# A macaron decoder trunk on one core: attention as a pipeline of score groups, with half of the last conv group's taps queued on VectorE behind the last window block's scaling

## Chip, core and metric

One core of a Trainium2 chip runs the whole program. The metric is the device time of one execution in microseconds. The profile's engines are PE (TensorE matmuls), PEld (TensorE weight loads), DVE (VectorE), ACT (ScalarE), POOL (GpSimd) and SP (the queue that issues most DMAs).

## What is computed

Two layers (L = 2) over a sequence of 512 tokens with 1024 channels. Each layer is a half-step feed-forward block, a mixer, and another half-step feed-forward block, each behind an RMS norm. Only the mixer is touched here:

```python
p = rms_norm(h) @ w_in                       # columns: conv (2 x 384), q (6 heads), k, v (2 heads), q_mem (4 heads)
u, gate = split(conv columns)
y_conv = silu(layer_norm(causal_depthwise_conv31(u * sigmoid(gate)) + b))
q, k = rope(rms_norm(q)), rope(rms_norm(k))
y_swa = softmax([q k^T / 8 + band mask, sink])[:-1] @ v     # sliding window of 128, in blocks of 128 queries
y_mem = softmax(rms_norm(q_mem) mk^T / 8) @ mv              # 256 memory tokens, mk and mv once per layer
h = h + concat(y_conv, y_swa, y_mem) @ w_out
```

## The kernel before

All data are float32. Large products are done as three fp32r products of a high and a low part (`mm3`, L172 to L174): the operand's high part is a copy by ScalarE (L141), its low part a subtraction by VectorE (L142). Small products (scores, probabilities by values, transposes) are plain fp32; a plain fp32 product appears on TensorE as two instructions, a transpose as one.

A tile framework records the operations of the source and orders them per engine by a timeline of its own; every engine then works through its own queue strictly in that order. `with queued():` and `tc.issue_after(x)` bind an instruction to stand behind `x` on its engine's queue; `tail[0]` holds the last TensorE instruction that such a binding refers to.

The mixer of a layer runs these steps (`ORDER`, L45), written in this order: `c0 c1 q v c2 r0 r1 w0 w1 w2 r2 w3 r3 t0 t1 t2 s`.

- `c` (`conv_in`, L631): for one of three groups of 128 conv channels, two projections of 24 matmuls of 512 columns (value half and gate half), then on VectorE the scaling by the RMS factor `R` and the gating into `ypad` (L646 to L649).
- `q` and `v` (`queries`, `values`): four tiles of 128 tokens each. For q, k and the memory queries a chain follows: ScalarE squares, VectorE sum of squares (L526), L527, GpSimd's power (L189), VectorE's scaling per head (L531), then transposes on TensorE (L555) and a copy by ScalarE (L557).
- `w` (`window`, L721) and `r` (`recall`, L740), one call for each block of 128 queries: a pair of heads at a time, scores (L728 and L745), the row minimum on VectorE (L731 with the mask added, L746 without), exponential with a sum of the row on ScalarE (L697), transposes of the probabilities (L702), a copy (L704), the product with the values (L707). At the end of a block the division by the sum (L713), transposes (L716) and the split into `y` (L141, L142). The keys of the two heads lie in one zero-padded tile (`kz`, `mz`), so that a score product has all 128 rows as contraction and 512 columns.
- `t` (`taps`, L752): for each group one tensor_scalar (L753) and 30 scalar_tensor_tensor operations of 128x512 (L756) on VectorE. The scheduler puts these between the other operations of VectorE.
- `s` (`swish`, L760): sum of the three groups on GpSimd (L762, L763), mean on TensorE (L765), its subtraction (L768), squares, their column sums on TensorE (L197), the power on GpSimd, its spreading over the tokens (L210), then scaling, Silu and split into `y[0]` to `y[2]`.

The output projection comes behind: eight blocks `d` of 15 matmuls that take the attention parts `y[3]` to `y[7]`, in eight PSUM banks, then eight blocks of 9 matmuls that take the conv parts, L794, and the next norm's operand. `whi` and `wlo` have four buffers each.

Of the kernel before, what the change touches and what calls it, by code (L numbers as in the profile page):

```python
# [18 lines left out]
P = 128  # L19
D = 1024  # L20
S = 512
# [22 lines left out]
MAGIC = 12582912.0  # L44
ORDER = "c0 c1 q v c2 r0 r1 w0 w1 w2 r2 w3 r3 t0 t1 t2 s"  # L45

# [13 lines left out]
def trunk(ctx: ExitStack, tc: tile.TileContext, xT, memT, pos, w1a, w3a, w2a, w1b, w3b, w2b,  # L60
# [15 lines left out]
    def queued():  # L76

        return tc.issue_after(tail[0].ins)
# [100 lines left out]
    def blk(k, n=P):  # L179
        return slice(k * n, (k + 1) * n)  # L180
# [89 lines left out]
    class Seven:  # L270
# [37 lines left out]
        def rest(self):  # L308
# [9 lines left out]
            self.cut(4, f)  # L318

    def gated():  # L320

        p = (gp.tile([P, 2, S], F32R, tag="ghi", name="ghi"), gp.tile([P, 2, S], F32R, tag="glo", name="glo"))
        return [at(p, ALL, i, ALL) for i in range(2)]
# [187 lines left out]

    mz = res.tile([P, 2, 2, MEM], F32, name="mz")
    for i in range(2):
        G.memset(mz[blk(1 - i, HD), :, i, :], 0.0)
    mvn = res.tile([P, 2, 256], F32, name="mvn")
    rmem = const.tile([P, 2], F32, name="rmem")
# [43 lines left out]
    def memory(l):  # L560
# [20 lines left out]
        for t in range(2):  # L581
            A.activation(mvn[:, t, :], pp[t][:, 256:512], AF.Copy, scale=rmem[:, t : t + 1])
# [5 lines left out]
            pt = to_columns(None, q, 2, "mm")  # L588
            for i in range(2):
                e = blk(i, HD)  # L590
                A.activation(mz[e, :, i, blk(t)], pt[e], AF.Copy, scale=-(HD**-0.5))

# [6 lines left out]
    def mixer(l, x, st, last):  # L599
# [6 lines left out]
        qT = here[:, 0:1536].rearrange("p (c s) -> p c s", c=CC)  # L606
        kz = here[:, 1536:2560].rearrange("p (i s) -> p i s", i=2)
        vn = here[:, 2560:3072].rearrange("p (t e) -> p t e", t=NT)
        qmT = there[:, 0:1024].rearrange("p (i s) -> p i s", i=2)
        cv = there[:, 1024:2560].rearrange("p (c s) -> p c s", c=CC)  # L610
        for i in range(2):
            G.memset(kz[blk(1 - i, HD), i, :], 0.0)
        scratch = [wst.tile([P, UNIT], F32, tag="aux", name=f"aux{i}", bufs=3) for i in range(3)]
# [11 lines left out]

        y = [z for _ in range(KD // 2) for z in gated()]


        R, rc = None, const.tile([P, NT], F32, tag="rc", name="rc")

        def conv_in(c):  # L631
            nonlocal R
            pp = []
            for i in range(2):
                with queued() if 2 * c + i < 3 else nullcontext():
                    ps = mm()
                    project(ps, weights(wconv[l, c, i], 1024, V), x)
                    pp.append(ps)
                if c == 0:
                    with queued():  # L640
                        if i == 0:
                            V.tensor_copy(rc, rms_cols(st, D))
                        else:
                            R = kept(spread(rc), "R")
            u, s = ypad[:, c, PAD:], ring("cv")
            V.tensor_tensor(out=u, in0=pp[0], in1=R, op=ALU.mult)  # L646
            V.tensor_tensor(out=s, in0=pp[1], in1=R, op=ALU.mult)
            A.activation(s, s, AF.Sigmoid)
            V.tensor_tensor(out=u, in0=u, in1=s, op=ALU.mult)  # L649


        def queries():
            ww = [weights(wqk[l, i], 1024, G) for i in range(4)]
            for t in range(NT):
# [18 lines left out]
                pt = to_columns(qT[:, :, blk(t)], q, 4)  # L673
                for i in range(2):
                    e = blk(i, HD)
                    A.activation(kz[e, i, blk(t)], pt[e, CC, :], AF.Copy, scale=-(HD**-0.5))


        def values():
            ww = [weights(wvm[l, i], 768, V) for i in range(4)]  # L680
            for t in range(NT):
                ps = mm()
                for k in range(KD):
                    mm3(ps[:, 0:CCH], at(x, ALL, k, blk(t)), at(ww[k // 2], ALL, blk(k % 2, CCH)), k == 0, k == KD - 1)
                A.activation(vn[:, t, :], ps[:, 256:CCH], AF.Copy, scale=rc[:, t : t + 1])
# [6 lines left out]
        def weighted(c, nk, scores, nm, den, values, po):  # L692

            pr = ring("pr").rearrange("p (i k) -> p i k", i=2)
            for i in range(2):
                n = 2 * c + i
                A.activation(pr[:, i, 0 : nk * P], scores[:, i, 0 : nk * P], AF.Exp, bias=nm[:, n : n + 1], scale=-1.0,  # L697
                             accum_out=den[:, n : n + 1])
            pt = bank([P, 2, 2, P], "pt")
            for i in range(2):  # L700
                for j in range(nk):
                    T.transpose(pt[:, i, j, :], pr[:, i, blk(j)], ident)  # L702
            ptb = ring("ptb").rearrange("p (i j q) -> p i j q", i=2, j=2)
            A.activation(ptb[:, :, 0:nk, :], pt[:, :, 0:nk, :], AF.Copy)  # L704
            for i in range(2):
                for j in range(nk):
                    T.matmul(po[:, 2 * c + i, :], ptb[:, i, j, :], values(j, i), start=(j == 0), stop=(j == nk - 1))  # L707

        def attended(b, c0, c1, po, rd):

            n = 2 * (c1 - c0)
            z = ring("yn")[:, 0 : (c1 - c0) * P]
            V.tensor_tensor(out=heads(z), in0=po, in1=rd.unsqueeze(2).to_broadcast([P, n, HD]), op=ALU.mult)  # L713
            pt = bank([P, c1 - c0, P], "cf")
            for c in range(c1 - c0):
                T.transpose(pt[:, c, :], z[:, blk(c)], ident)  # L716
            for c in range(c1 - c0):
                hi, lo = at(y[CC + c0 + c], ALL, blk(b))
                split(hi, lo, pt[:, c, :], V)

        def window(b):  # L721
            nk = 2 if b else 1
            b0, W = b - nk + 1, nk * P
            nm, es, den, rd = (sm(NH, f"a{n}", "a", 12) for n in range(4))
            po = bank([P, NH, HD], "po")
            for c in range(CC):
                ps = bank([P, 2, 256], "mm")
                T.matmul(ps[:, :, 0:W], qT[:, c, blk(b)], kz[:, :, b0 * P : b0 * P + W], start=True, stop=True)  # L728
                for i in range(2):
                    n = 2 * c + i  # L730
                    V.tensor_tensor_reduce(out=ps[:, i, 0:W], in0=ps[:, i, 0:W], in1=mask[:, 256 - W : 256], scale=1.0,  # L731
                                           scalar=nsink[:, l, n : n + 1], op0=ALU.add, op1=ALU.min, accum_out=nm[:, n : n + 1])
                weighted(c, nk, ps, nm, den, lambda j, i: vn[:, b0 + j, blk(i, HD)], po)
            V.tensor_tensor(out=es, in0=sink, in1=nm, op=ALU.add)
            A.activation(es, es, AF.Exp)
            V.tensor_tensor(out=den, in0=den, in1=es, op=ALU.add)
            V.reciprocal(rd, den)
            attended(b, 0, CC, po, rd)

        def recall(b):  # L740
            nm, den, rd = (sm(NM, f"m{n}", "a", 12) for n in range(3))
            po = bank([P, NM, HD], "po")
            for c in range(2):
                ps = bank([P, 2, 256], "mm")
                T.matmul(ps, qmT[:, c, blk(b)], mz[:, c], start=True, stop=True)  # L745
                V.tensor_reduce(out=nm[:, 2 * c : 2 * c + 2], in_=ps, axis=AX.X, op=ALU.min)  # L746
                weighted(c, 2, ps, nm, den, lambda j, i: mvn[:, j, blk(2 * c + i, HD)], po)
            V.reciprocal(rd, den)
            attended(b, CC, CC + 2, po, rd)


        def taps(c):  # L752
            V.tensor_scalar(out=cv[:, c, :], in0=ypad[:, c, 0:S], scalar1=conv_w[:, c, 0:1], scalar2=conv_b[:, c : c + 1],  # L753
                            op0=ALU.mult, op1=ALU.add)
            for j in range(1, TAPS):
                V.scalar_tensor_tensor(out=cv[:, c, :], in0=ypad[:, c, j : j + S], scalar=conv_w[:, c, j : j + 1],  # L756
                                       in1=cv[:, c, :], op0=ALU.mult, op1=ALU.add)

# [19 lines left out]
        for step in ORDER.split():  # L778
            f = {"c": conv_in, "q": queries, "v": values, "w": window, "r": recall, "t": taps, "s": swish}[step[0]]
            f(*map(int, step[1:]))  # L780
# [141 lines left out]
```

## Time and profile before

| quantity | value |
|---|---|
| median of 3 runs | 1829.91 us (1829.8 to 1833.07) |
| profiled execution | 1829.19 us |
| its span | 1827.4 us, mean granted TensorE clock 0.993 |
| busy: PE, PEld, DVE, ACT, POOL | 97%, 86%, 72%, 49%, 10% of the span |
| mixer of the first layer, values to the end of attention | 442.9 to 516.4 us |
| mixer of the second layer, the same | 1344.4 to 1415.3 us |

The profiled execution is 1.8 us longer than its span (work around the span) and 0.7 us under the median. Rows of the timeline read: start, duration, engine, source line, operation, output <- inputs, shape, count; in brackets the idle time of the engine ahead of the row and what ended it. Rows overlap, since an instruction starts before the one ahead of it has left the pipeline; what an instruction costs its engine is therefore the distance from start to start.

### The profile page before, as it was taken

What the parts mean: (1) busy time and instruction counts of PE and PEld (TensorE: products, weight loads), DVE (VectorE), ACT (ScalarE), POOL (GpSimd) and SP (SyncE); (2) the same over time, 40 slices, a digit from 0 to 9 for tenths busy, and PEclk for the clock granted to TensorE, in tenths of its full rate; (3) what the DMA queues carried; (4) which work ended last, traced back from release to release, by engine and by line L of the source; (5) the groups of instructions that cost most, each with busy time, mean ns of one, the idle gap of its engine ahead of it and who ended that gap; (6) DMA issues with size and microseconds to landing.
All of it is one profiled execution on the core that took longest, in us unless ns stands there. A gap on an engine that the chain in (4) does not pass through costs nothing.

```text
span 1827.4 us, 28061 instructions
## 1 busy us (share of the span) xinstructions
PE 1773.5 (97%) x10892; PEld 1579.3 (86%) x10892; DVE 1306.6 (72%) x1990; ACT 887.8 (49%) x1453; POOL 177.8 (10%) x182
## 2 busy tenths in 40 slices
PE   8999999999899999999999999999988999999997
PEld 6889999878577989898888898988776889898986
DVE  8967666579957867576678685666799477675755
ACT  4546444354646535353555463535356455353532
POOL 3001000014101000000010010000240010000000
PEclk9999999999999999999999999999999999999998
DMA  7356655162038456565565475643420576474622
GB/s 244 105 171 171 166 138 151 53 170 76 8 91 204 103 152 160 142 169 142 147 141 153 147 177 138 168 119 102 109 83 13 135 161 162 133 180 122 172 76 81
DMA packets 91285, 243.63 MB, mean 133 GB/s; under 512 B 9360, under 2 KB 11664, under 8 KB 91152
## 3 DMA queue, kind: packets, MB, share of 16 engines
q1 hardware_dynamic: 77040, 190.45, 34.0%
q0 software_dynamic: 14112, 51.39, 15.9%
q8 instruction: 86, 1.41, 0.3%
q14 instruction: 47, 0.39, 0.1%
HBM read 239.70 MB, written 2.10 MB: 132 GB/s over the span
## 4 chain that ended last, share of the span: by engine, by line
PE 77%; DVE 11%; issue 7%; DMA 2%; ACT 2%; POOL 0%; SPq 0%; DVEq 0%; POOLq 0%; ACTq 0%
PE mm L172 11%; PE mm L173 11%; PE mm L174 11%; PE po L172 8%; PE po L173 8%; PE po L174 8%; PE pt L173 5%; PE pt L172 5%; PE pt L174 5%; DVE there L756 4%; DVE wlo L142 1%; DMA wsum<-in_w3b 1%; DVE mm L731 1%; DVE xlo L152 1%; PE cf L172 1%
## 5 line engine op out<-in xcount | busy, mean ns | idle before, releaser
L141 ACT ACTIVATE whi<-raw 128x1024 fp32r<-128x1024 f32 (+4 forms) x384 | 353.1, 924 | 514.1 <-PE mm L173 248.1
L142 DVE TENSOR_TENSOR wlo<-raw,whi 128x1024 fp32r<-128x1024 f32 (+4 forms) x384 | 404.6, 1056 | 128.0 <-ACT whi L141 127.0
L173 PE MATMUL mm<-glo,whi 128*128 128x512 f32 x752 | 294.1, 391 | 0.0
L174 PE MATMUL mm<-ghi,wlo 128*128 128x512 f32 x752 | 293.4, 390 | 0.0
L172 PE MATMUL mm<-ghi,whi 128*128 128x512 f32 x752 | 289.8, 392 | 0.8 <-ACT ghi L141 0.8
L174 PE MATMUL po<-mh,wlo 128*128 128x256 f32 x864 | 244.6, 283 | 1.3 <-DVE wlo L142 1.3
L172 PE MATMUL pt<-xhi,whi 128*128 128x256 f32 x864 | 243.3, 283 | 2.7 <-ACT xhi L141 2.0
L172 PE MATMUL po<-mh,whi 128*128 128x256 f32 x864 | 244.8, 283 | 0.8 <-ACT part L377 0.8
L173 PE MATMUL pt<-xlo,whi 128*128 128x256 f32 x864 | 243.7, 283 | 1.5 <-DVE xlo L142 1.5
L173 PE MATMUL po<-ml,whi 128*128 128x256 f32 x864 | 244.6, 283 | 0.0
L174 PE MATMUL pt<-xhi,wlo 128*128 128x256 f32 x864 | 243.7, 283 | 0.0
L455 DVE SCALAR_TENSOR_TENSOR h<-mm,h 128x512 f32<-128x512 f32 x128 | 87.8, 688 | 139.1 <-PE mm L174 139.0
L172 PEld LDWEIGHTS pt<-xhi,whi 128*128 128x128 f32 x864 | 165.1, 192 | 4.2 <-ACT xhi L141 2.4
L172 PEld LDWEIGHTS mm<-ghi,whi 128*128 128x128 f32 x752 | 141.6, 189 | 30.6 <-ACT ghi L141 1.3
L173 PEld LDWEIGHTS pt<-xlo,whi 128*128 128x128 f32 x864 | 165.7, 192 | 2.5 <-DVE xlo L142 1.7
L172 PEld LDWEIGHTS po<-mh,whi 128*128 128x128 f32 x864 | 165.8, 192 | 1.8 <-ACT part L377 1.2
L174 PEld LDWEIGHTS po<-mh,wlo 128*128 128x128 f32 x864 | 165.8, 192 | 1.6 <-DVE wlo L142 1.6
L174 PEld LDWEIGHTS mm<-ghi,wlo 128*128 128x128 f32 x752 | 141.6, 188 | 29.4
L173 PEld LDWEIGHTS po<-ml,whi 128*128 128x128 f32 x864 | 165.8, 192 | 0.6
L173 PEld LDWEIGHTS mm<-glo,whi 128*128 128x128 f32 x752 | 141.7, 188 | 28.3 <-DVE glo L142 0.4
L174 PEld LDWEIGHTS pt<-xhi,wlo 128*128 128x128 f32 x864 | 165.5, 192 | 0.0
L756 DVE SCALAR_TENSOR_TENSOR there<-ypad,par,there 128x512 f32<-128x512 f32 x180 | 134.1, 761 | 0.7
(271 smaller groups left out, 3256.4 us busy)
## 6 DMA issues: line engine op xcount, KB each, us to landing
raw<-in_w2a SPq DMA_DIRECT2D x48, 384.0 KB, 3.5
raw<-in_w2b SPq DMA_DIRECT2D x48, 384.0 KB, 3.8
raw<-in_w1b SPq DMA_DIRECT2D x26, 512.0 KB, 3.7
raw<-in_w3b SPq DMA_DIRECT2D x26, 512.0 KB, 3.7
raw<-in_w1a SPq DMA_DIRECT2D x25, 512.0 KB, 3.7
raw<-in_w3a SPq DMA_DIRECT2D x25, 512.0 KB, 4.1
wsum<-in_w1a SPq DMA_DIRECT2D x18, 512.0 KB, 4.5
wsum<-in_w3a SPq DMA_DIRECT2D x18, 512.0 KB, 4.6
```

What stands on the lines that cost most here:

```text
L141: A.activation(hi, x, AF.Copy)
L142: on.tensor_tensor(out=lo, in0=x, in1=hi.bitcast(F32), op=ALU.subtract)
L152: V.scalar_tensor_tensor(out=lo, in0=x, scalar=col, in1=hi.bitcast(F32), op0=ALU.mult, op1=ALU.subtract)
L172: T.matmul(ps, a[0], b[0], start=first, stop=False, **more)
L173: T.matmul(ps, a[0], b[1], start=False, stop=False, **more)
L174: tail[0] = T.matmul(ps, a[1], b[0], start=False, stop=last, **more)
L455: V.scalar_tensor_tensor(out=h[:, d, :], in0=ps, scalar=0.5, in1=h[:, d, :], op0=ALU.mult, op1=ALU.add)
L731: V.tensor_tensor_reduce(out=ps[:, i, 0:W], in0=ps[:, i, 0:W], in1=mask[:, 256 - W : 256], scale=1.0, scalar=nsink[:, l, n : n + 1], op0=A ...
L756: V.scalar_tensor_tensor(out=cv[:, c, :], in0=ypad[:, c, j : j + S], scalar=conv_w[:, c, j : j + 1], in1=cv[:, c, :], op0=ALU.mult, op1=AL ...
```

## The change

The conv group 2 and all of `w` and `r` become one step `a` (`attention`), so `ORDER` is `c0 c1 q v a t0 t1 t2 s`.

- The eight calls become ten groups (`GROUPS`) of one to three head pairs. `scored` makes the scores of a whole group, one ahead of the group that is being turned; `turned` does exponentials, transposes and copy of a pair; the product with the values (`weighted`) comes one pair late; the transposes of a finished block (`attended`) come one group late. All TensorE instructions of attention are bound to stand in written order.
- Keys are no longer zero-padded: a head's score product contracts over 64 rows (partitions 0 to 63 or 64 to 127) with 256 columns, and the two heads of a pair write to different PSUM banks (`mm`, `mm` or `cf`).
- The window mask is added by a matmul of the identity with the mask in fp32r (L724) into the score bank ahead of the scores. The row minimum of a group is one tensor_reduce for each head of the pair (L745, L734), and the sink enters by two small operations (L746, L747).
- The sum of a row comes from a column of ones behind the values (65 columns instead of 64), not from the exponential's accumulator.
- Conv group 2 is projected inside attention: its first half (24 matmuls, in a `po` bank) behind the first group's scores, its second half behind the second group's.
- The split of the attention output takes two channel blocks at once where it can.
- In `taps`, the operations 15 to 30 of group 2 are bound behind `scaling["w"]`, the division of the last window block.

```diff
-ORDER = "c0 c1 q v c2 r0 r1 w0 w1 w2 r2 w3 r3 t0 t1 t2 s"
+ORDER = "c0 c1 q v a t0 t1 t2 s"
...
+        def conv_half(c, i):
...
+            ps = bank([P, S], "po") if c == 2 else mm()
+            with queued() if c == 2 or 2 * c + i < 3 else nullcontext():
+                project(ps, weights(wconv[l, c, i], 1024, V), x)
...
+        def scored(kind, pairs):
...
+            pp = [mm()[:, 0 : n * W].rearrange("p (n k) -> p n k", n=n) for _ in range(2)]
+            masked = kind == "w"
+            with queued():
+                if masked:
+                    for ps in pp:
+                        T.matmul(ps, identr, maskr[:, 256 - W : 256].unsqueeze(1).to_broadcast([P, n, W]), start=True, stop=False,
+                                 skip_group_check=True)
+                for z, (b, c) in enumerate(pairs):
+                    for i in range(2):
+                        e = blk(i, HD)
+                        q, k = (qT[e, c, blk(b)], kT[e, (b + 1) * P - W : (b + 1) * P]) if masked else (qmT[e, c, blk(b)], mT[e, c, :])
+                        tail[0] = T.matmul(pp[i][:, z, :], q, k, start=not masked, stop=True, skip_group_check=True)
...
+        GROUPS = (("r", (0, 0), (0, 1)), ("r", (1, 0), (1, 1)), ("w", (0, 0), (0, 1), (0, 2)), ("w", (1, 0), (1, 1)), ("w", (2, 0), (2, 1)),
+                  ("w", (1, 2), (2, 2)), ("r", (2, 0), (2, 1)), ("w", (3, 0), (3, 1)), ("w", (3, 2)), ("r", (3, 0), (3, 1)))
...
+            s = scored(GROUPS[0][0], GROUPS[0][1:])
+            for n, (kind, *pairs) in enumerate(GROUPS):
+                ready = list(done)
+                done.clear()
+                if n < 2:
+                    conv_half(2, n)
+                nxt_s = None
+                if 2 <= n + 1 < len(GROUPS):
+                    nxt_s = scored(GROUPS[n + 1][0], GROUPS[n + 1][1:])
+                for z, (b, c) in enumerate(pairs):
+                    x = turned(kind, b, c, [ps[:, z, :] for ps in s[0]], s[1])
+                    close()
+                    late = (kind, b, c, *x)
+                if n == 0:
+                    nxt_s = scored(GROUPS[1][0], GROUPS[1][1:])
+                s = nxt_s
+                for r in ready:
+                    attended(*r)
...
             for j in range(1, TAPS):
-                V.scalar_tensor_tensor(out=cv[:, c, :], in0=ypad[:, c, j : j + S], scalar=conv_w[:, c, j : j + 1],
-                                       in1=cv[:, c, :], op0=ALU.mult, op1=ALU.add)
+
+                with tc.issue_after(scaling["w"].ins) if c == CC - 1 and j >= TAPS // 2 else nullcontext():
+                    V.scalar_tensor_tensor(out=cv[:, c, :], in0=ypad[:, c, j : j + S], scalar=conv_w[:, c, j : j + 1],
+                                           in1=cv[:, c, :], op0=ALU.mult, op1=ALU.add)
```

Outside the mixers the instructions stay as they were, but for a few neighbours that trade places. Three places of the first layer's order matter to the prediction; the second layer has the same order there.

The first is PE's queue where the values' projection ends (`cf<-whi,xlo`). Before, the transposes of the last query tile (`pt<-cst,gg`) are followed there by conv group 2 (`mm<-xhi,whi`, and so on, 48 in all) and only then by the transposes of the memory queries (`po<-cst,gg`) and the first scores (`mm<-mz,there`):

```order
L555 MATMUL pt<-cst,gg 128x128 x4
L174 MATMUL cf<-whi,xlo 128x384
L172 MATMUL mm<-xhi,whi 128x512
...
L174 MATMUL mm<-xhi,wlo 128x512
L555 MATMUL pt<-cst,gg 128x128 x4
L555 MATMUL po<-cst,gg 128x128 x2
L745 MATMUL mm<-mz,there 128x512 x2
```

Now:

```order
L561 MATMUL pt<-cst,gg 128x128 x4
L174 MATMUL cf<-whi,xlo 128x384
L561 MATMUL pt<-cst,gg 128x128 x4
L561 MATMUL po<-cst,gg 128x128 x2
L730 MATMUL mm<-mT,there 128x256 x4
L561 MATMUL po<-cst,gg 128x128 x6
L172 MATMUL po<-xhi,whi 128x512
```

All eight transposes of memory queries (four tiles, two each) and the first group's scores now stand ahead of conv group 2.

The second is DVE's queue behind the last window block's division (L713 before, L786 now; `there<-ypad,par,there` is a tap, `glo` the attention output's low part, `wlo` a weight's). Before, no tap is left there:

```order
L713 TENSOR_TENSOR aux_3742<-po,a_4708 128x384
L748 RECIPROCAL m_4775<-m_4774 128x4
L142 TENSOR_TENSOR glo<-cf,ghi 128x128 x2
L768 SCALAR_TENSOR_TENSOR there<-pt,there 128x512 x3
```

Now:

```order
L786 TENSOR_TENSOR aux_3740<-po,rd_4767 128x384
L857 SCALAR_TENSOR_TENSOR there<-ypad,par,there 128x512 x2
L784 RECIPROCAL rd_4789<-po 128x4
...
L857 SCALAR_TENSOR_TENSOR there<-ypad,par,there 128x512 x8
L142 TENSOR_TENSOR wlo<-raw,whi 128x640
...
L142 TENSOR_TENSOR wlo<-raw,whi 128x384
L869 SCALAR_TENSOR_TENSOR there<-pt,there 128x512 x3
```

Sixteen taps and five weight splits now stand between the division and the subtraction of the conv mean (L768 before, L869 now).

The third is PE's queue around the conv mean (L765 before, L866 now) and the column sums of the squares (L197). Before, with the last attention transposes (`cf<-cst,aux`) and output projection matmuls between:

```order
L765 MATMUL pt<-aux_3743,onesq 128x512
L707 MATMUL po<-mvn,aux_3741 128x64 x4
L716 MATMUL cf<-cst,aux_3742 128x128 x3
L172 MATMUL mm<-ghi,whi 128x512 x3
...
L197 MATMUL cf<-onesq,st 128x1
```

Now:

```order
L174 MATMUL po<-ghi,wlo 128x512
L866 MATMUL pt<-aux_3741,onesq 128x512
L197 MATMUL cf<-onesq,st 128x1
```

The mean moved behind 75 matmuls of the output projection, and the column sums stand right behind it.

More of the change, by code (lines that the diff above doesn't have):

```diff
@@ L318, in rest, with gated_pair @@
             self.cut(4, f)
+    def gated_pair():
+        return (gp.tile([P, 2, S], F32R, tag="ghi", name="ghi"), gp.tile([P, 2, S], F32R, tag="glo", name="glo"))
     def gated():
-        p = (gp.tile([P, 2, S], F32R, tag="ghi", name="ghi"), gp.tile([P, 2, S], F32R, tag="glo", name="glo"))
+        p = gated_pair()
         return [at(p, ALL, i, ALL) for i in range(2)]
@@ L509, in rope_tables @@
         A.activation(cs, z, AF.Sin)
[L512 to L515, printed above, removed]
+    mT = res.tile([P, 2, MEM], F32, name="mT")
+    mvn = res.tile([P, 2, NM, HD + 1], F32, name="mvn")
+    G.memset(mvn[:, :, :, HD : HD + 1], 1.0)
+    maskr = res.tile([P, P + 256], F32R, name="maskr")
+    A.activation(maskr, cst[:, 0 : P + 256], AF.Copy)
+    identr, maskr = maskr[:, 0:P], maskr[:, P : P + 256]
     rmem = const.tile([P, 2], F32, name="rmem")
@@ L587, in memory @@
             V.tensor_tensor(out=heads(q), in0=heads(q), in1=gmem.unsqueeze(1).to_broadcast([P, NM, HD]), op=ALU.mult)
[L588 to L591, printed above, removed]
+            A.activation(mT[:, :, blk(t)], to_columns(None, q, 2, "mm"), AF.Copy, scale=-(HD**-0.5))
     def prepare(l):
@@ L699, in weighted @@
             pt = bank([P, 2, 2, P], "pt")
-            for i in range(2):
-                for j in range(nk):
-                    T.transpose(pt[:, i, j, :], pr[:, i, blk(j)], ident)
+            with queued():
+                for i in range(2):
+                    for j in range(nk):
+                        tail[0] = T.transpose(pt[:, i, j, :], pr[:, i, blk(j)], ident)
             ptb = ring("ptb").rearrange("p (i j q) -> p i j q", i=2, j=2)
             A.activation(ptb[:, :, 0:nk, :], pt[:, :, 0:nk, :], AF.Copy)
-            for i in range(2):
-                for j in range(nk):
-                    T.matmul(po[:, 2 * c + i, :], ptb[:, i, j, :], values(j, i), start=(j == 0), stop=(j == nk - 1))
@@ L709, in attended @@
[L709 to L728, printed above, removed]
-                for i in range(2):
[L730 to L749, printed above, removed]
+            return ptb, nk
@@ new lines, in weighted, with scaled @@
+        def weighted(kind, b, c, ptb, nk, po):
+            with queued():
+                for i in range(2):
+                    for j in range(nk):
+                        v = vn[:, b - nk + 1 + j, i, :] if kind == "w" else mvn[:, j, 2 * c + i, :]
+                        tail[0] = T.matmul(po[:, 2 * c + i, :], ptb[:, i, j, :], v, start=(j == 0), stop=(j == nk - 1))
+        def scaled(kind, b, po):
+            n = NH if kind == "w" else NM
+            rd = sm(n, f"rd{n}", "a", 4)
+            if kind == "w":
+                e = esw[:, b]
+                A.activation(e, e, AF.Exp)
+                V.tensor_tensor(out=rd.rearrange("p (c i) -> p i c", i=2), in0=po[:, :, HD].rearrange("p (c i) -> p i c", i=2), in1=e, op=ALU.add)
+                V.reciprocal(rd, rd)
+            else:
+                V.reciprocal(rd, po[:, :, HD])
+            z = ring("yn")[:, 0 : n * HD]
+            scaling[kind] = V.tensor_tensor(out=heads(z), in0=po[:, :, 0:HD], in1=rd.unsqueeze(2).to_broadcast([P, n, HD]), op=ALU.mult)
+            return z
@@ new lines, in mixer, with attended @@
+        scaling = {}
+        def attended(kind, b, z):
+            n = CC if kind == "w" else 2
+            pt = bank([P, n, P], "pt")
+            with queued():
+                for c in range(n):
+                    tail[0] = T.transpose(pt[:, c, :], z[:, blk(c)], ident)
+            c = 0
+            while c < n:
+                k = CC + c + (0 if kind == "w" else CC)
+                m = 2 - k % 2
+                hi, lo = at(yy[k // 2], ALL, slice(k % 2, 2), blk(b))
+                split(hi, lo, pt[:, c : c + m, :], V)
+                c += m
@@ L778, in mixer @@
         for step in ORDER.split():
-            f = {"c": conv_in, "q": queries, "v": values, "w": window, "r": recall, "t": taps, "s": swish}[step[0]]
+            f = {"c": conv_in, "q": queries, "v": values, "a": attention, "t": taps, "s": swish}[step[0]]
             f(*map(int, step[1:]))
```

109 lines of the change are left out of this document (79 added, 30 removed).

## The prediction

> **What bounds the kernel now.** I read the busy times of the page first, then the windows of the stages, then the timelines of PE and DVE in the first mixer.
>
> ```profile
> PE 1773.5 (97%) x10892; PEld 1579.3 (86%) x10892; DVE 1306.6 (72%) x1990; ACT 887.8 (49%) x1453; POOL 177.8 (10%) x182
> ...
> core 0: us, PE busy (x) PEld busy (x) DVE busy (x) ACT busy (x) POOL busy (x), PEclk, DMA share, GB/s
> 442.90:516.40 73.50, 63.06 (x345) 45.11 (x343) 70.67 (x175) 43.23 (x145) 10.77 (x7) 0.95 0.09 28
> 516.40:547.10 30.70, 30.70 (x147) 25.53 (x148) 11.15 (x22) 11.89 (x22) 2.85 (x3) 1.00 0.51 129
> 1344.40:1415.30 70.90, 59.83 (x344) 44.66 (x343) 67.99 (x173) 43.90 (x146) 10.63 (x7) 0.98 0.13 36
> ```
>
> PE is nearly full over the whole span, so only a stage in which it waits has time to give. In the attention of both layers (first and third window) DVE is full and PE has some 10 us idle at a granted clock of 0.95 and 0.98. Behind it, in the output projection, PE is full and DVE a third busy. So the change moves DVE work out of the one place where DVE is the bound. What decides is whether PE is then fed earlier, or has its own queue in the way.
>
> ```profile
> 442.67 0.42 PE L174 MATMUL cf<-whi,xlo 128*128 128x384 f32 x1
> 443.63 0.50 PE L172 MATMUL mm<-xhi,whi 128*128 128x512 f32 x1 [0.54 <-ACT hsq L524]
> ...
> 458.24 1.98 PE L745 MATMUL mm<-mz,there 128*128 128x512 f32 x4 [1.95 <-ACT there L557]
> 461.04 0.89 PE L702 MATMUL pt<-cst,uu 128*128 128x128 f32 x4 [0.81 <-ACT uu L697]
> ...
> 463.81 3.52 PE L745 MATMUL mm<-mz,there 128*128 128x512 f32 x4
> 467.12 0.80 PE L728 MATMUL mm<-here 128*128 128x256 f32 x2
> ...
> 484.73 1.15 PE L702 MATMUL pt<-cst,uu 128*128 128x128 f32 x4 [4.91 <-ACT uu L697]
> ...
> 516.39 0.98 PE L172 MATMUL mm<-ghi,whi 128*128 128x512 f32 x3 [0.44 <-ACT ghi L141]
> ...
> 1415.28 0.97 PE L172 MATMUL mm<-ghi,whi 128*128 128x512 f32 x3 [0.37 <-ACT ghi L141]
> ```
>
> The reader is to see what PE does from 443.63 on: conv group 2, the only long work that needs nothing from DVE, starts as soon as the values' projection ends, and hides DVE's work on the memory queries. Its waits come afterwards. The output projection starts at 516.39 and 1415.28; these are the ends that I compute anew.
>
> **Conv group 2 starts late.** In the new PE queue all transposes of the memory queries stand ahead of conv group 2. The last two need the scaling of tile 3 (L531, L537 now) on DVE. DVE's queue is the same up to the first L527 of the memory queries:
>
> ```profile
> 452.33 0.15 DVE L527 TENSOR_SCALAR hv<-hs 128x4 f32<-128x4 f32 x1
> ...
> 455.06 0.40 DVE L526 TENSOR_REDUCE hs<-hsq 128x4 f32<-128x256 f32 x1
> 455.39 0.40 DVE L531 TENSOR_TENSOR gg<-gg,rsq 128x256 f32<-128x256 f32 x1
> 455.72 0.73 DVE L756 SCALAR_TENSOR_TENSOR there<-ypad,par,there 128x512 f32<-128x512 f32 x1
> 456.38 0.67 DVE L647 TENSOR_TENSOR aux<-mm,R 128x512 f32<-128x512 f32 x1
> ...
> 468.13 0.67 DVE L746 TENSOR_REDUCE m<-mm 128x2 f32<-128x512 f32 x1
> 468.73 0.73 DVE L756 SCALAR_TENSOR_TENSOR there<-ypad,par,there 128x512 f32<-128x512 f32 x1
> ...
> 1351.83 0.16 DVE L527 TENSOR_SCALAR hv<-hs 128x4 f32<-128x4 f32 x1
> ```
>
> From start to start (455.06, 455.39, 455.72, 456.38) a sum of squares or a scaling costs 0.33, a tap 0.66; a minimum 0.60 (468.13 to 468.73); an L527 0.07. Between 452.40 and the end of that last scaling the new queue has 9 taps (5.9), 3 sums (1.0), 4 scalings (1.3), 3 L527 (0.2) and the first group's 2 minima (1.2): 9.7, so it ends at 462.1 and conv group 2 starts at 462.6 instead of 443.63. GpSimd's powers fit between (two DVE operations or more lie there each time). PE idles most of those 19 us; only transposes and four first scores lie in them.
>
> **PE's work from there to the end of attention.** The prices:
>
> ```profile
> 498.24 1.90 PE L707 MATMUL po<-here,aux 128*128 128x64 f32 x16
> 499.97 0.61 PE L702 MATMUL pt<-cst,uu 128*128 128x128 f32 x4
> 500.41 1.02 PE L728 MATMUL mm<-here 128*128 128x512 f32 x2
> 501.27 0.60 PE L702 MATMUL pt<-cst,pr 128*128 128x128 f32 x4
> ...
> 540.17 0.39 PE L172 MATMUL pt<-ghi,whi 128*128 128x512 f32 x1
> ...
> 544.02 0.39 PE L174 MATMUL pt<-ghi,wlo 128*128 128x512 f32 x1
> ```
>
> From start to start: 16 of the 64-column instructions take 1.73, 0.108 each; four transposes 0.44, 0.11 each; a 512-column fp32 instruction 0.43; an fp32r one 0.227 (3.85 over 17).
> - Conv group 2: 48 x 0.227 = 10.9.
> - Masks, which are new on PE: 5376 columns, 10.5 x 0.227 = 2.4.
> - Scores without the first group's: before, 32 + 42 products of 512 and 256 columns make 15.9; halved in contraction and width, twice as many instructions of 256 columns at half of 0.43, the same 15.9; less the first group's 1.7, 14.2.
> - 94 transposes x 0.11 = 10.3; 148 instructions of probabilities by values x 0.108 = 16.0 (the 65th column adds 0.2).
>
> Together 53.8. Cold restarts: at 463.81 four instructions took 3.31 from start to start where 1.72 is the rule, 1.6 lost; the granted clock of 0.95 over 73.5 us bounds all loss at 3.7. After a longer idle I take 2.3, between the two. Waits inside the pipelined groups: from 0 to the 4.91 at 484.73; I take 1.6, twice the 0.81 at 461.04, since scores run a group ahead. The end is 462.6 + 57.7 = 520.3, 3.9 later than 516.39. In layer 1, from the same steps from 1351.83 (9.7 and the 0.5 to the first matmul) give 1351.9 + 10.2 + 57.7 = 1419.8, 4.5 late.
>
> A rule of the Trainium skill, "TensorE: Matmul & The Clock Gate", Part 3 (Packing small matmuls), says that products in different row groups run at the same time in the array. By it alternating heads on rows 0 to 63 and 64 to 127 would halve the scores, 7.1 us less per layer. Against it stands "TensorEngine Tiling (Array Packing)", Key Properties: changing the tiling mode drains TensorE, at each turn from 64 rows to 128. No run here shows either yet.
>
> No row has a 64-row product. Below, the full 14.2 is halved at most (-7.1); but a second instruction of the same head that follows has the same rows, and of each run of eight slots five can overlap, which gives -5.3. Above, each of about 20 changes between the two kinds could cost 0.1 (a transpose), +2.0. I take half of the overlap, -2.7 per layer, as nothing tells the ends apart.
>
> **The taps behind the division.** 16 taps of 0.66, 10.6 us, leave the attention's DVE queue; fewer minima and splits free some 3 more. After 462 DVE has less work than PE, so this isn't on the path. Behind the division they delay the output's low parts, which the first projection matmuls need: one tap's rest, 0.5 per layer. Their last one and GpSimd's sum (1.27, below) come about 16.5 us after the end of attention; the 75 matmuls now ahead of the conv mean cover 17.1. If that cover fails, PE stalls tap for tap.
>
> **The conv mean loses its cover.**
>
> ```profile
> 508.00 1.27 POOL L763 TENSOR_TENSOR aux<-aux,there 128x512 f32<-128x512 f32 x1 [27.53 <-DVE a L734]
> ...
> 513.70 1.08 PE L765 MATMUL pt<-aux,onesq 128*128 128x512 f32 x2
> ...
> 514.81 1.89 DVE L768 SCALAR_TENSOR_TENSOR there<-pt,there 128x512 f32<-128x512 f32 x3 [0.92 <-PE pt L765]
> ...
> 517.15 0.68 DVE L240 TENSOR_TENSOR st<-st,sq 128x512 f32<-128x512 f32 x1
> ...
> 525.84 0.28 PE L197 MATMUL cf<-onesq,st 128*128 128x1 f32 x2
> ```
>
> From the mean's start (513.70) to the last sum of squares (517.15 + 0.68) it is 4.1 us; before, PE did other products until 525.84. Now the column sums stand right behind the mean: PE stalls 4.1 - 0.9 = 3.2, and 0.3 for the bank, 3.5 per layer. The chain behind it to the first conv product keeps 45 matmuls, 10.2 us; I add nothing.
>
> **Sum.** 3.9 + 4.5 + 2 x (0.5 + 3.5) - 2 x 2.7 = +11.0, on the profiled 1829.19: 1840.2; the median lies 0.7 above that execution, so 1841.
>
> **Rivals.**
> - *Full overlap of the scores.* -5.3 to -7.1 per layer and no waits (-1.6): 16.4 - 10.6 = +5.8 down to 16.4 - 17.4 = -1.0: 1829 to 1836. For it speaks that heads alternate and have banks of their own; against it, that every row of this trace shows a matmul behind the one before.
> - *No overlap, and the changes cost.* +16.4 and up to 4.0 more: 1846 to 1851. Its sign is a 256-column score at 0.215 or more.
> - *VectorE's relief decides: faster.* If conv group 2 finds its way to PE early, DVE's 70.67 of 73.50 is the bound and 13.6 fall away, less the 4.0 behind attention: -9.6 per layer, 1811. The point from which it decides: conv group 2 must start 5.5 us earlier than I say (half of the sum, 11.0), by 457. For it: the full DVE window. Against it: the 9 taps stand ahead of the scaling in the queue, and DVE has no gap there to give.
> - *The taps aren't covered.* If 75 matmuls end before GpSimd's sum, up to 2 us more per layer; it lies in the ranges above.
>
> **How the numbers follow.** The forecast (1836 to 1846) has 0.42, full overlap 0.20, no overlap 0.18, the relief 0.20. The likeliest gives 1841. The range 1818 to 1852 holds the first three and a quarter of the relief's cases, 0.85, less the tails of the sum's other terms. A measurement of this kernel tells 0.2%, 3.7 us, from no change. Faster (under 1826): 0.20, the relief; the same: 0.14, most of full overlap; slower (over 1833.6): 0.66.
>
> **What would show it.** In the profile after: the first conv product into a `po` bank at 462 to 463, with PE's wait before it ended by DVE's scaling; the first output projection product at 517 to 520; an idle of some 3 us at L197 in both layers; a score's start-to-start between 0.11 and 0.215. Wrong, if conv group 2 starts before 457, if L197 waits under 1 us, or if PE waits inside the groups for exponentials more than 5 us in all.

## The result

The changed kernel takes 1861.03 us (median of 4 runs, 1859.03 to 1861.75) beside 1831.49 us before (4 runs): the ratio is 1.015, 95% interval 1.0128 to 1.0171. It is slower, as forecast, but by 29.5 us instead of 11, outside the range. The profiled execution took 1859.03 us, its span 1857.1, against 1829.19 and 1827.4.

The page's busy times and the windows of the first layer's mixer after the change (window, length, busy time of PE, PEld, DVE, ACT, POOL, granted clock, DMA):

```profile
PE 1779.8 (96%) x10996; PEld 1590.6 (86%) x10996; DVE 1304.2 (70%) x1918; ACT 880.2 (47%) x1350; POOL 170.6 (9%) x179
...
core 0: us, PE busy (x) PEld busy (x) DVE busy (x) ACT busy (x) POOL busy (x), PEclk, DMA share, GB/s
440.90:460.50 19.60, 5.74 (x22) 3.40 (x22) 19.57 (x39) 8.57 (x21) 7.29 (x5) 0.56 0.23 67
460.50:516.50 56.00, 53.30 (x374) 43.59 (x372) 38.23 (x86) 31.83 (x76) 1.29 (x1) 0.97 0.04 13
516.50:537.60 21.10, 18.37 (x79) 14.53 (x79) 16.81 (x27) 6.08 (x10) 3.08 (x3) 1.00 0.62 153
537.60:547.20 9.60, 9.31 (x40) 7.95 (x40) 0.47 (x2) 0.52 (x1) 1.03 (x1) 0.64 0.01 2
547.20:570.70 23.50, 23.50 (x106) 19.39 (x105) 14.65 (x26) 14.60 (x24) 0.92 (x1) 1.00 0.51 145
570.70:582.80 12.10, 7.38 (x32) 4.73 (x30) 9.39 (x13) 10.87 (x15) 2.12 (x3) 1.00 0.76 199
```

PE is nearly idle up to 460.5 (5.74 of 19.60 us) and full up to the end of attention; DVE has room there now (38.23 of 56.00). New are the third, fourth and last window: idle time on PE in the output projection, a stretch of 9.6 us at a granted clock of 0.64, and 4.7 us of idle time at the next norm. Before, the projection had PE full at 1.00.

To see where the time went, four marks of PE's timeline serve: a product of the feed-forward block ahead, the first product of the output projection, the next norm's column sums, a product of the block behind. Before (the projection's first products are in the prediction):

```profile
355.30 0.40 PE L172 MATMUL mm<-ghi,whi 128*128 128x512 f32 x1
...
570.51 1.05 PE L197 MATMUL cf<-onesq,st 128*128 128x1 f32 x8
...
646.54 0.40 PE L172 MATMUL mm<-ghi,whi 128*128 128x512 f32 x1
```

After:

```profile
353.21 0.40 PE L172 MATMUL mm<-ghi,whi 128*128 128x512 f32 x1
...
516.48 0.96 PE L172 MATMUL mm<-ghi,whi 128*128 128x512 f32 x3 [0.37 <-ACT ghi L141]
...
581.93 1.05 PE L197 MATMUL cf<-onesq,st 128*128 128x1 f32 x8 [2.16 <-DVE st L240]
...
659.56 0.40 PE L172 MATMUL mm<-ghi,whi 128*128 128x512 f32 x1
```

| stage | layer 0 before, after | layer 1 before, after | longer by |
|---|---|---|---|
| up to the end of attention | 161.09, 163.27 | 159.90, 161.86 | 2.2, 2.0 |
| output projection to the norm's sums | 54.12, 65.45 | 54.84, 65.90 | 11.3, 11.1 |
| norm's sums to the block behind | 76.03, 77.63 | 76.03, 77.64 | 1.6, 1.6 |

That is 29.7 us before rounding, all of what the span grew by; outside these stages 2.1 us less ahead of the first mixer stand against 1.0 more between the mixers and 1.0 more behind the second. Attention, which the change rebuilds, costs 2 us per layer. The loss lies behind it.

**Attention.**

```profile
459.90 0.66 PE L561 MATMUL po<-cst,gg 128*128 128x128 f32 x2 [1.61 <-DVE gg L537]
460.21 0.78 PE L172 MATMUL po<-xhi,whi 128*128 128x512 f32 x1
...
469.74 0.48 PE L730 MATMUL mm<-mT,there 64*128 64x256 f32 x1
469.74 0.48 PE L730 MATMUL cf<-mT,there 64*128 64x256 f32 x1
470.06 0.38 PE L730 MATMUL mm<-mT,there 64*128 64x256 f32 x1
470.06 0.38 PE L730 MATMUL cf<-mT,there 64*128 64x256 f32 x1
```

Conv group 2 starts at 460.21, right behind the last memory query's transposes, which DVE's scaling released: the mechanism of the forecast. The two heads of a pair start at the same time, one in `mm`, one in `cf`: score products on different halves of the rows run together. The first pair of a group takes 0.32 to the next, later pairs 0.21 (0.215 is what the forecast took for one of them alone), so the change of kind costs some 0.1. It needs no change of rows: behind the 128-row transposes of L210 (546.36) the first 512-column product also takes 0.32 to the next (547.17 to 547.49), where 0.23 is the rule.

**The conv mean and what follows it.**

```profile
533.85 1.02 PE L866 MATMUL pt<-aux,onesq 128*128 128x512 f32 x2
537.63 0.38 PE L197 MATMUL cf<-onesq,st 128*128 128x1 f32 x2 [2.77 <-DVE st L240]
...
540.39 0.80 PE L172 MATMUL cf<-ghi,whi 128*128 128x512 f32 x1 [0.25 <-DVE ms L203]
...
545.25 0.59 PE L174 MATMUL cf<-ghi,wlo 128*128 128x512 f32 x1
545.68 0.40 PE L172 MATMUL cf<-ghi,whi 128*128 128x512 f32 x1
...
529.95 1.29 POOL L864 TENSOR_TENSOR aux<-aux,there 128x512 f32<-128x512 f32 x1 [6.62 <-DVE there L857]
```

GpSimd's sum ends at 531.24, PE reaches the mean at 533.85: the 16 taps themselves are covered. PE then waits 2.77 and 0.25. Behind the wait products take 0.43 from start to start (545.25 to 545.68), not 0.227, for 12 products (the first takes 0.60): 2.6 more. The column sums take 2.5 instead of 1.7, and the mean, which lay ahead of the projection before, adds its 1.0. Together 7.4 in the first layer.

**The next norm.** DVE's additions to `h` (first and last of eight), before and then after:

```profile
549.21 0.69 DVE L794 TENSOR_TENSOR h<-mm,h 128x512 f32<-128x512 f32 x1 [1.15 <-PE mm L174]
...
564.89 0.68 DVE L794 TENSOR_TENSOR h<-pt,h 128x512 f32<-128x512 f32 x1
```

```profile
560.86 0.69 DVE L895 TENSOR_TENSOR h<-mm,h 128x512 f32<-128x512 f32 x1 [5.02 <-PE mm L174]
...
574.14 0.68 DVE L895 TENSOR_TENSOR h<-pt,h 128x512 f32<-128x512 f32 x1
...
571.88 0.50 PE L174 MATMUL mm<-xhi,wlo 128*128 128x512 f32 x1 [0.86 <-DVE wlo L142]
...
576.14 0.50 PE L173 MATMUL mm<-xlo,whi 128*128 128x512 f32 x1 [0.74 <-DVE xlo L152]
...
578.25 0.50 PE L172 MATMUL mm<-xhi,whi 128*128 128x512 f32 x1 [0.68 <-ACT xhi L151]
```

Seen from the projection's first product (516.39 and 516.48), the first addition is 11.6 us later, the last 9.2; 7.4 of this is the projection's own delay. In the new PE queue the conv parts of the first four blocks alternate between their banks, and then those of three more, so blocks end in bunches and DVE does additions, weight splits and operand splits all at once. PE, by then in the next feed-forward block, waits for the operand: 4.7 us where it was 0.9 before, 3.8 more, 2.16 of it at 581.93; behind that it runs at half pace once more, from 583.5 to 586.5 in the first layer (the 1.6 of the table's last row).

### The profile page after: what moved, and what is told of

Its sections match the earlier page's. It is cut to its first block, busy times and chain, and to the rows that moved or that the text cites. A ratio compares the mean times of both kernels' runs of the same rounds, so it can differ in the third digit from the quotient of the medians.

```text
span 1857.1 us, 28078 instructions
## 1 busy us (share of the span) xinstructions
PE 1779.8 (96%) x10996; PEld 1590.6 (86%) x10996; DVE 1304.2 (70%) x1918; ACT 880.2 (47%) x1350; POOL 170.6 (9%) x179
## 4 chain that ended last, share of the span: by engine, by line
PE 79%; DVE 10%; issue 7%; DMA 2%; ACT 2%; SPq 0%; DVEq 0%; POOLq 0%; POOL 0%; ACTq 0%
PE mm L172 11%; PE mm L173 10%; PE mm L174 10%; PE po L172 9%; PE po L173 9%; PE po L174 9%; PE pt L172 5%; PE pt L173 5%; PE pt L174 5%; DVE there L857 4%; DVE wlo L142 2%; PE po L772 1%; DVE st L240 1%; DVE xlo L152 1%; PE cf L197 1%
```

## Experiments

Ratios are against the kernel before, with 95% intervals. Changes are against the changed kernel unless said.

### The taps free again

```diff
-with tc.issue_after(scaling["w"].ins) if c == CC - 1 and j >= TAPS // 2 else nullcontext():
+with tc.issue_after(scaling["w"].ins) if c == CC - 1 and j >= 99 else nullcontext():
```

`j` ends at 30, so no tap is bound.

> The changed kernel with the 16 taps of group 2 no longer bound behind the last window block's division; the pipelined attention stays. On PE's queue the conv mean then stands behind 12 output projection products instead of 75, 32 products lie between it and the column sums, and the conv parts of the projection follow block by block. Theory A (the loss lies behind attention and comes from the order that the late taps set: 3.0 us of stall at the column sums, 3.4 of cold clock behind it, 5.6 from conv parts that interleave their banks): the stall and the interleaving go, attention still ends some 2 us late per layer, so 1832 to 1838. Theory B (VectorE's load in attention decides, the order behind it is cheap): 16 taps, 10.6 us per layer, are back in attention, which ends that much later; 1855 to 1865.

1.0028 (1.0015 to 1.004), 1836.82 us: theory A. The binding of the taps costs nearly all of it. PE around the mean:

```profile
520.59 1.02 PE L866 MATMUL pt<-aux,onesq 128*128 128x512 f32 x2
...
528.71 0.28 PE L197 MATMUL cf<-onesq,st 128*128 128x1 f32 x2
```

No wait at the sums. With 16 taps back in attention its end comes 3.2 and 2.7 us later than in the kernel before, one or less later than with the taps bound (163.27 becomes 164.30): DVE had the room.

### The binding alone, on the kernel before

```diff
+with tc.issue_after(scaling[0].ins) if c == CC - 1 and j >= TAPS // 2 else nullcontext():
     V.scalar_tensor_tensor(out=cv[:, c, :], ...)
```

> The kernel before with one thing changed: taps 15 to 30 of group 2 bound behind the last window block's division, as in the changed kernel; the attention stays the old one. On PE's queue the conv mean again stands behind 75 projection products with the column sums right behind it, and the conv parts interleave. Theory A (the binding costs about 12 us per layer behind attention, whatever the attention): attention ends 3 to 6 us earlier per layer through VectorE's relief, the rest is lost as in the changed kernel: 1841 to 1850. Theory B (the loss needs the pipelined attention): 1820 to 1830.

1.0129 (1.0106 to 1.0152), 1855.77 us: theory A in kind, 6 us above its range.

```profile
512.97 0.96 PE L172 MATMUL mm<-ghi,whi 128*128 128x512 f32 x3 [0.37 <-ACT ghi L141]
...
530.54 1.02 PE L768 MATMUL pt<-aux,onesq 128*128 128x512 f32 x2
536.01 0.59 PE L197 MATMUL cf<-onesq,st 128*128 128x1 f32 x2 [4.45 <-DVE st L240]
```

The profiled execution is the slowest of the four, 1861.09 us. Attention ends 2.0 and 3.3 us earlier per layer: this is what VectorE's relief is worth to the old attention. Behind it the sums wait 4.45 us and the projection takes 69.5 us instead of 54.1. The loss needs no pipelined attention.

### Half of the taps bound

`j >= 23` instead of `j >= TAPS // 2`.

> The changed kernel with 8 taps instead of 16 bound behind the division. On PE's queue the conv mean then stands behind 45 projection products, 30 products (6.8 us) lie between it and the column sums, and the conv parts still interleave. Theory A: the stall of 3.0 and the cold clock of 3.4 per layer go, the waits at the next norm stay: 1846 to 1851. Theory B (what is lost is the total of VectorE's work behind attention): half of the loss, near 1845, and the waits at the next norm halve too.

1.0097 (1.008 to 1.0115), 1849.43 us: within theory A's range. The mean starts at 527.12, the sums at 534.80 without a wait, and the waits of 2.16 at the next norm are still there. The stage of the projection shrinks by 6.0 and 5.5 us; the one behind it grows by 1.6 and 1.5, since the half pace behind the norm's sums lasts longer.

### The conv parts block by block

```diff
-mm3(oo[d], at(w, ALL, blk(n)), y[n], False, n == CC - 1)
+with queued():
+    mm3(oo[d], at(w, ALL, blk(n)), y[n], False, n == CC - 1)
```

> The changed kernel with the 72 conv-part products of the output projection bound in written order, nine per block, as the kernel before has them; taps and conv mean as in the changed kernel. Theory A (interleaved blocks end in bunches, so the residual sums and the next norm's operand come late: 3.8 us of waits and 1.8 of cold clock per layer): 11 us less, 1848 to 1852, with the stall at the conv mean unchanged. Theory B (the interleaving only fills time in which the last conv channels aren't there yet): no change, 1858 to 1863, and new waits for the conv channels on PE.

1.0133 (1.0115 to 1.0151), 1855.4 us: between the theories. The stage from the projection to the norm's sums shrinks by 3.0 and 2.3 us, the one behind it by 1.6 in the first layer and grows by 1.6 in the second, 5.3 in all instead of 11. The wait of 2.16 at the norm's sums is gone in both layers. The half pace is gone in the first only: in the second, behind waits of 0.28, 1.50, 0.29 and 0.30 ahead of the norm's sums, the granted clock is 0.50 from 1492.58 to 1497.50. So the bunching is real, and smaller than I had put it: the conv channels themselves arrive late.

### Both mended, 8 taps still bound

The two edits above together.

> The changed kernel with 8 taps instead of 16 bound behind the division, and the conv-part products of the output projection bound block by block. On PE's queue 30 products lie between the conv mean and the column sums. Theory A (what the binding costs is the missing cover at the column sums and the interleaved blocks, not VectorE's work itself): both are mended though 8 taps stay behind attention, so it comes near the kernel without the binding, 1833 to 1841. Theory B (VectorE's late work costs time for each tap): half of what the binding costs, 1843 to 1850.

1.0057 (1.0041 to 1.0072), 1842.43 us: just above theory A's range and below B's. By the ratios (1.015 and 1.0057) the cover and the order give back 17 of 27 us though 8 taps stay behind attention; some 5 us over the kernel without the binding remain. I put them down to L210, and with it all conv channels, still coming 5 us later against the first projection product (23.9 after it, 18.5 there); no run shows this by itself.

### Conv group 2 ahead of attention

```diff
-            ps = bank([P, S], "po") if c == 2 else mm()
+            ps = mm()
...
-            if c == 2:
-                gate(c, i)
...
+            conv_in(2)
             s = scored(GROUPS[0][0], GROUPS[0][1:])
...
-                if n < 2:
-                    conv_half(2, n)
```

> The changed kernel with conv group 2 projected ahead of attention, behind the values as in the kernel before, in the mm banks; all else stays. Theory A (PE idles about 14 us per layer because conv group 2 stands behind the memory queries' transposes): its 10.9 us fill that idle time and attention ends 8 to 11 us earlier per layer: 1839 to 1846, the losses behind attention unchanged. Theory B (once PE is fed, VectorE's chain of maxima and copies bounds attention): at most 3 us per layer, 1854 to 1860.

1.0153 (1.0137 to 1.017), 1859.22 us: no gain, and not for theory B's reason. Windows of the first layer:

```profile
453.50:465.00 11.50, 6.01 (x29) 3.49 (x27) 11.50 (x24) 7.87 (x17) 3.52 (x3) 0.66 0.19 57
465.00:485.00 20.00, 17.98 (x81) 14.46 (x81) 17.40 (x34) 6.38 (x18) 2.03 (x2) 0.50 0.00 1
485.00:517.20 32.20, 31.21 (x239) 25.98 (x238) 17.50 (x48) 20.09 (x52) 0.00 (x0) 0.96 0.00 1
```

From 465 to 485 PE is 90% busy at a granted clock of 0.50: half of these 18 busy microseconds, 9 of the 10.9 that conv group 2 had filled, are lost again. Short waits alone don't explain it: the last of them ends at 474.50, and from 475 to 487 PE is busy without a gap, still at 0.50. The attention of the first layer ends as late as in the changed kernel (163.4 and 163.3 us behind the first mark), that of the second 2.5 us earlier; the stages behind it take some 2.6 us more in each layer of this execution. In the changed kernel conv group 2, in the middle of attention, brings the clock back: products are 0.23 apart again from 464 on, 4 us after it starts.

### Half of conv group 2 ahead of attention, taps free

> The changed kernel without the binding of the taps, and with the first half of conv group 2 (24 products) ahead of attention, the second half behind the first group's scores. Theory A (24 products, 5.5 us, fill idle time of PE): attention ends 4 to 5.5 us earlier per layer: 1823 to 1828. Theory B (the clock decides: after the first half PE waits again, the granted clock falls to 0.5 and stays there as it does for 20 us in the kernel with all of conv group 2 first, since the short waits inside the groups don't let it rise): 1832 to 1840.

1.003 (1.0012 to 1.0048), 1835.64 us: theory B by the time. Its mechanism shows in the first layer alone, where the clock from 462 to 490 is 0.74 (0.96 with the taps free and conv group 2 in its place) and attention ends 0.7 us later than there; in the second the clock is 0.95 from 1365 to 1393 and attention ends 3.3 us earlier.

### Taps out of the way of the memory queries

```diff
-tc.issue_after(scaling["w"].ins) if c == CC - 1 and j >= TAPS // 2
+tc.issue_after(scaling["q"].ins) if c == 1 and j >= 16    # scaling of the last memory query tile
```

> The changed kernel without the binding of group 2's taps; instead taps 16 to 30 of group 1 are bound behind the scaling of the last memory query tile, so that 7 of the 9 taps that stood ahead of it move behind. Theory A (those taps hold the scaling, the transposes and with them conv group 2 back): conv group 2 starts 4 to 5 us earlier in each layer and attention ends as much earlier: 1823 to 1828. Theory B (the taps only move, and hold back the first groups' minima and exponentials instead): 1832 to 1837.

0.9993 (0.9983 to 1.0004), 1831.37 us: some 6 us better than with free taps alone, about half of theory A's gain. Conv group 2 starts at 458.41 and 1358.84 where the kernel with free taps and without this binding has 460.75 and 1362.20; against the mark in the block ahead that is 2.4 and 2.6 us earlier, and attention ends 2.8 and 2.5 us earlier. It is as fast as the kernel before, no faster.

### Both: conv group 2 first, those taps late, group 2's taps free

> The changed kernel with group 2's taps free, conv group 2 ahead of attention and taps 16 to 30 of group 1 bound behind the last memory query's scaling. Theory A (with conv group 2 first, the granted clock stayed at 0.5 for 20 us because PE waited again and again for that scaling; with the taps out of its way the waits go and the clock stays up): attention ends 6 to 10 us earlier per layer, 1812 to 1822. Theory B (the clock falls anyway at the first groups' waits for minima and exponentials): 1827 to 1836.

0.9963 (0.995 to 0.9975), 1826.83 us beside 1833.11: faster than both kernels, less than theory A had it. First layer:

```profile
441.00:462.00 21.00, 16.56 (x83) 12.62 (x82) 20.01 (x43) 11.55 (x27) 10.16 (x5) 0.99 0.31 95
462.00:490.00 28.00, 24.01 (x139) 18.63 (x139) 27.24 (x53) 12.06 (x31) 1.79 (x1) 0.76 0.00 1
...
482.52 1.11 PE L761 MATMUL pt<-cst,uu 128*128 128x128 f32 x4 [3.35 <-ACT uu L755]
```

The clock holds up to 462 and falls later, with DVE full (27.24 of 28.00) and PE waiting 3.35 us for an exponential. Attention ends 2.1 and 2.9 us earlier than before.

### The same, the taps behind the second group's minima

> As the run with conv group 2 first and late taps, but the 15 taps are bound behind the second group's minima instead of the scaling. Theory A (taps ahead of those minima hold the second group back): some 2 us per layer better than that run. Theory B (that group is hidden behind the first one's transposes and products): the same within 2 us in all.

0.9977 (0.9965 to 0.9989), 1828.13 us: theory B, no better.

### Conv group 2 in its place, taps behind those minima, conv parts in order

> The changed kernel with group 2's taps free, conv group 2 where the change has it, taps 16 to 30 of group 1 bound behind the second group's minima, and the conv-part products bound block by block. Theory A (conv group 2's start is set by VectorE's queue ahead of the scaling): conv group 2 starts near 455, attention ends some 5 us earlier than in the kernel without bindings, 1823 to 1828. Theory B (taps moved that far back make the conv mean late again): 1830 to 1838.

1.0108 (1.009 to 1.0126), 1853.72 us: a miss for both theories. Conv group 2 starts at 459.99, which is 105.0 us behind the mark in the block ahead: 2.4 us earlier than with the taps free, and no earlier than with the taps behind the last scaling (104.9). With no tap left between the last scalings, DVE now waits for GpSimd's powers (0.34 to 0.55 before each of the last three) and PE for ScalarE's copies (1.04 and 0.32). The first layer's attention takes as long as with the taps free (164.4 and 164.3 us), the second's 13.7 us longer: the moved taps fill DVE's queue late in attention. Why the first layer escapes this stays open. Second layer:

```profile
1400.00:1420.00 20.00, 14.08 (x99) 11.39 (x97) 19.79 (x38) 8.04 (x21) 1.27 (x1) 0.91 0.00 1
1420.00:1440.00 20.00, 17.55 (x84) 15.77 (x84) 10.85 (x28) 7.75 (x20) 1.26 (x1) 0.55 0.00 1
```

PE starves while DVE is full, then runs the last 20 us at 0.55.

### The heads one after the other

```diff
-for z, (b, c) in enumerate(pairs):
-    for i in range(2):
+for i in range(2):
+    for z, (b, c) in enumerate(pairs):
```

> The changed kernel with the score products of a group issued head by head (all pairs of the lower 64 rows, then all pairs of the upper 64) instead of alternating; nothing else moves. Theory A (two score products run at once only where neighbours on the queue use different halves of the rows): the overlap is left at the border between the heads alone, scores cost 4 to 7 us more per layer, 1868 to 1876, and the timeline shows starts 0.1 to 0.2 apart where they are 0.01 apart now. Theory B (TensorE looks ahead far enough to pair them): 1858 to 1863.

1.0151 (1.0131 to 1.017), 1859.36 us: theory B. On the timeline, in the second group, heads still start in pairs:

```profile
470.12 0.48 PE L730 MATMUL mm<-mT,there 64*128 64x256 f32 x1
470.13 0.48 PE L730 MATMUL cf<-mT,there 64*128 64x256 f32 x1
```

In this kernel's queue all products of the lower rows stand ahead of those of the upper rows (four instructions here), yet the first of both start together. Attention takes as long as in the changed kernel (163.5 and 162.3 us, 163.3 and 161.9 there).

## Right and wrong, step by step

- *Conv group 2 starts late*: right. Forecast 462.6, measured 460.21 in an execution whose first layer ran 2.1 us earlier (353.21 against 355.30), so 462.3 on the old scale. Taking 7 taps out of its way brought 2.4 and 2.6 us.
- *Attention's end*: forecast +1.2 and +1.8 per layer with half of the overlap, measured +2.2 and +2.0. The parts were off. The scores overlap fully, which is the mechanism of the first rival: both heads of a pair start at 469.74. The Trainium skill, "TensorE: Matmul & The Clock Gate", Part 3, has products in different row groups run at once; the trace agrees with that. The changes of kind cost about 0.1 each, my upper bound. Waits on the groups' inputs came to 2.3 us (0.25, 0.61, 1.12 and 0.29) where I took 1.6. From the start of conv group 2 to the projection it is 56.3 us (460.21 to 516.48), 55.0 by the forecast. So the overlap that I left out was spent again on other terms, and that the end came out within 1 us is in part luck.
- *The taps behind the division*: the cover held (531.24 against 533.85); the 0.5 for the late low parts didn't show, since the first products went through with 0.37 of wait, as before.
- *The conv mean loses its cover*: the wait was right (3.2 + 0.3 forecast, 2.77 + 0.25 measured). The step that failed is its price: I counted the wait alone, subtracted the mean's own time, and left out the granted clock behind it. Measured 7.4, not 3.5: the waits 3.0, the mean's own time 1.0, the slow clock 3.4 (0.8 in the column sums, 2.6 in the products behind).
- *"The chain behind it ... I add nothing"*: the second failure, and the larger one. The late conv channels change the order of the projection's last 72 products and delay the residual additions by 8 to 12 us, 7.4 of it the projection's own lag; that returned, in the first layer, as 3.8 us of waits and 1.6 us of slow clock at the next norm, where I had put nothing. The old and new queues had shown both orders; I read them around the mean only.
- *Rivals*: "relief decides" fell: binding the taps on the old attention moved its end by 2.0 and 3.3 us only. "No overlap" had the nearest time, for a wrong reason.

By the runs, the binding costs some 22 us (ratios 1.015 and 1.0028 of 1832) and the pipelined attention some 5 us (1.0028). Shown: the cover (with 8 taps fewer) and the order of the projection's end, mended one by one and together. Not separated by a run of its own: the share of the slow clock in each stall; it is read from the timeline.

## What to carry to other kernels

Work moved off an engine's busy stage lands in the chain that the next stage hangs on: follow it to the next norm, not to the first engine that covers it. A tensor engine's stall costs the stall and the slow clock behind it; here 3 us brought 3.4 more. In a kernel whose scheduler sets the order, one binding moves instructions far behind it: compare the queues up to the next point where all work joins.

## What the runs showed of the hardware

- Score products of two heads on different halves of the rows start within 0.02 us of each other and take 0.21 per pair of instructions, even where the source binds four instructions of one head ahead of the other's.
- The granted clock doesn't rise with busy time alone: with conv group 2 first, 20 us at 90% busy stayed at 0.50 while PE ran transposes and small products, and from 475 to 487 without a wait. In the changed kernel conv products brought it back within 4 us (460.21 to 463.76). The Trainium skill ("TensorE: Matmul & The Clock Gate", Part 1) has some 3.4 us of sustained work for that; the trace agrees for the conv products and not for the attention's small ones. What the clock counts was not tried.
- A wait of 2.77 us with 16 one-column products behind it was enough to halve the pace: it fell between 1.1 and 1.5 us after the wait, within these products, and stayed so for the next 12. In the run with the conv parts block by block a longest wait of 1.50 us went ahead of 4.9 us at 0.50.
